# When the plain weight piece of a first-ff tile is prepared, how activations are read back, and how many dots go with a piece

## The chip, the cores and the metric

The kernel runs on one core of a Trainium2 chip. The metric is the device time of one execution in microseconds (us). Engines are named as in the profile: PE is TensorE, DVE is VectorE, ACT is ScalarE, POOL is GpSimd, SP is SyncE, which issues most of the DMAs.

## What is computed

One layer of a diffusion backbone: a half-step SwiGLU feed-forward (ff), token mixing (attention beside a long convolution), and a second half-step feed-forward, each behind an RMS norm with shift, scale and gate from a conditioning vector. The change touches the first ff, which runs on 256 latent and 256 context tokens together, and the shifts, scales and gates (the "modulation") that are worked out meanwhile. Cut to that:

```python
D_MODEL = 2048; SEQ = 256; CTX_LEN = 256; D_FF = 5632; N_MOD = 9

def swiglu(h, w_up, w_down):
    gate, up = jnp.split(h @ w_up, 2, axis=-1)
    return (jax.nn.silu(gate) * up) @ w_down

def half_ffn(s, m, slot, g, w_up, w_down):
    h = modulate(rms_norm(s, g), chunk(m, 3 * slot), chunk(m, 3 * slot + 1))
    return s + 0.5 * chunk(m, 3 * slot + 2) * swiglu(h, w_up, w_down)

mod = (s_lat @ w_ada[l] + b_ada[l])[:, None, :]
mod_c = (s_ctx @ w_ada[l] + b_ada[l])[:, None, :]
x = half_ffn(x, mod, 0, g_norm[l, 0], w_ffn1_up[l], w_ffn1_down[l])
ctx = half_ffn(ctx, mod_c, 0, g_norm[l, 0], w_ffn1_up[l], w_ffn1_down[l])
```

## The kernel before

**Precision.** Every fp32 operand x is split into a rounded part hi and the rest lo = x - hi. A product is three matmuls: hi by hi, hi by lo, lo by hi (mm3, lines 239 to 241). Weights are split as they arrive: ACT casts hi, DVE subtracts (weight(), L228 and L232; split_to(), L208 and L209).

**The up stage (Ffn.up, L445).** The 5632 columns of the first ff are 44 tiles of 128 (gate and up together). Tiles 0 to 2 are made beside the start of the kernel; the change concerns tiles 3 to 43, made one after another. A tile takes four weight pieces kq = 0 to 3 of 512 KB, four of the 16 blocks of rows each. Piece 0 is always plain: 8 products, so 24 matmuls of 512 columns. Pieces 3, 2 and 1 become "quads" from tiles 5, 7 and 9 on (QUADS): there the product of 2 x 2 blocks is made by a scheme of seven products (in place of eight) of 256 columns, 14 a piece, so 42 matmuls of 256 columns. Such a piece is split in two halves (three and four of the combined blocks), with three sums on DVE between them (L425 to L427); whi and wlo have three buffers each, raw weights four.

Piece 0 is split differently (prepare(), L412 to L420). For each half ACT casts hi (L417) and writes -hi into lo (L418), and a DMA on POOL adds the raw weight to lo in memory (L419). So DVE is not used for it. Its four result tiles come from the tag "u", a pool of 58 tiles of 256 KB that also holds the activations h (32 of them), their sums for the quads, and the results of each tile.

When a tile's products are done, they are combined and go through SiLU (L467 to L475, ACT and DVE). keep() then writes the result to memory in two parts: ACT makes a copy and its negative (L481, L482), and POOL issues two writes and an adding write (L483 to L485). All these tiles are "u" tiles too. In up(), w = self.prepare(j, kq) stands right before the matmuls of the piece:

```python
            for kq in range(4):
                w = w or self.prepare(j, kq)
                for bank, part, n, q, block, x in todo[kq]:
```

**The dots (ada_dve, L133 to L148).** The modulation needs w_ada times the conditioning vectors: 224 dots beside this ff, each a 512 KB load on SP (L141) and one multiply-and-sum on DVE (L145), or two where the context needs it too. They are dealt out by hook(): each call adds a rate to an account, and a dot is issued for each whole unit. In the up stage the hook is called after each piece (rate 0.79, from tile 4 on), in the down stage before each step (rate 1.25).

**The down stage (Ffn.down, L519).** The 44 result tiles are 11 groups of four; the 2048 output columns are 8 pieces in two passes of four. A step is one group by one piece: one weight load, one split, 24 matmuls of 512 columns. Before the four steps of a group, fetch() (L487) issues all reads of the groups up to two ahead: eight DMAs of 256 KB on POOL for each group not yet held. At most five groups are held (ROOM). In pass 1 the first steps use groups held from pass 0. The last two groups of pass 1 are made separately for the two token sets.

**Order.** The program's order is a scheduler's input: it puts instructions in the order of the program on their engines, lets later ones pass where an earlier one isn't ready, and gives buffers out tag by tag. Every engine then works through its own line in that order.

Of the kernel before, what the change touches and what calls it, by code (L numbers as in the profile page):

```python
# [12 lines left out]
F32R = mybir.dt.float32r  # L13
# [5 lines left out]
P = 128  # L19
D = 2048  # L20
KT = D // P
L = 256
FF = 5632
JT = FF // P
GRP = 4
# [6 lines left out]
WAVE = 3  # L32
ADA_UP = (5, 7, 6, 8)
ADA_DOWN = (2, 3, 4)
ADA_RATES = (0.79, 1.25)
QUADS = {3: 5, 2: 7, 1: 9}
GT = JT // GRP
PASSES = ((0, 1, 2, 3), (4, 5, 6, 7))
ORDERS = ((9, 8, 10, 7, 6, 5, 4, 3, 2, 1, 0), tuple(range(GT)))
ROOM = 5  # L40
# [22 lines left out]
def hybrid_layer_kernel(ctx: ExitStack, tc: tile.TileContext, a):  # L63
    nc = tc.nc
# [3 lines left out]
    def T(pool, shape, tag, dt=F32, bufs=None):  # L68
        serial[0] += 1
        kw = {} if bufs is None else {"bufs": bufs}  # L70
        return pool.tile(list(shape), dt, tag=tag, name=f"{tag}_{serial[0]}", **kw)
# [3 lines left out]
    up = ctx.enter_context(tc.tile_pool(name="up", bufs=1))  # L75
    pp = ctx.enter_context(tc.tile_pool(name="pp", bufs=4, space=PSUM))

    def U(shape, dt=F32):
        return T(up, shape, "u", dt, 58)

    def tmp(shape):
        return T(up, shape, "sq", bufs=2)

    def tmp2(shape):
        return T(up, shape, "sg", bufs=3)
# [99 lines left out]
    def ada_col(d):  # L185

        bank = ada_bank.pop(d)
        rows = tmp2((P, 2 * P))
        copied = S.copy(rows, bank[:, 0 : 2 * P])
        for j in range(2):  # L190
            last = PE.transpose(bank[:, (2 + j) * P : (3 + j) * P], rows[:, j * P : (j + 1) * P], ident)
        col = cols[d % 2]
        turned = bank[:, 2 * P : 4 * P].rearrange("p (j g c) -> p j c g", g=4, c=32)
        V.tensor_reduce(col, turned[:, :, 0:2, :], axis=AX.X, op=ALU.add)
        V.scalar_tensor_tensor(first_mod[:, 1, d, :], col[:, 0, :], bada1[:, d : d + 1],
                               gn[:, 0, d : d + 1].broadcast_to((P, 2)), op0=ALU.add, op1=ALU.mult)
        V.tensor_scalar(first_mod[:, 0, d, :], col[:, 1, :], bada[:, d : d + 1], None, op0=ALU.add)
        return copied, last, bank
# [39 lines left out]
    def mm3(ps, w, xx, start, stop):  # L238
        PE.matmul(ps, w[0], xx[0], start=start, stop=False)  # L239
        PE.matmul(ps, w[0], xx[1], start=False, stop=False)  # L240
        return PE.matmul(ps, w[1], xx[0], start=False, stop=stop)  # L241
# [110 lines left out]
    class Ffn:  # L352
# [89 lines left out]
                    for bank, part, block, term in terms:  # L442
                        yield bank, part, n, q, block, (2 * kq + q, term)

        def up(self, j, w=None):  # L445
            todo = [list(self.products(j, kq)) for kq in range(4)]
            left = [sum(t[0] == bank for piece in todo for t in piece) for bank in range(4)]
            total = list(left)
            banks = [(PA, PB)[j % 2]((P, 2, L)) if n else None for n in left]
            for kq in range(4):  # L450
                w = w or self.prepare(j, kq)
                for bank, part, n, q, block, x in todo[kq]:
                    ps = banks[bank] if part is None else banks[bank][:, part, :]
                    xx = self.h[x] if part is None else self.sums[x[0]][x[1]]
                    left[bank] -= 1
                    mm3(ps, [t[q][:, block] if kq == 0 else t[:, q, block] for t in w[n]], xx, left[bank] == total[bank] - 1, left[bank] == 0)
                w = None
                if j == JT - 1 and kq == 1:
                    self.fetch(ORDERS[0][0])
                self.hook()  # L460
            for kq in QUADS:
                if QUADS[kq] == j + 1:
                    self.install(kq)
            if not total[2]:
                return self.close(j, banks)
            g, v, u = tmp((P, 2, L)), U((P, 2, L)), T(up, (P, L), "mt", bufs=3)
            S.copy(g[:, 0, :], banks[2][:, 0, :])  # L467
            V.tensor_add(u, g[:, 0, :], banks[2][:, 1, :])
            V.tensor_add(g[:, 1, :], u, banks[3][:, 0, :])
            V.tensor_add(v[:, 0, :], u, banks[3][:, 1, :])  # L470
            V.tensor_add(v[:, 1, :], g[:, 1, :], banks[3][:, 1, :])
            V.tensor_add(g, g, banks[0])
            V.tensor_add(v, v, banks[1])
            S.activation(g, g, AF.Silu)
            V.tensor_mul(v, v, g)  # L475
            self.keep(j, v)
# [7 lines left out]
            nc.gpsimd.dma_start(actd[j][:, 1], minus)  # L484
            nc.gpsimd.dma_start(actd[j][:, 1], act.bitcast(F32R), accum_op=ALU.add)  # L485

        def fetch(self, g):  # L487

            if g not in self.held:
                self.held[g] = []  # L490
                for j in range(g * GRP, (g + 1) * GRP):
                    act = U((P, 2, L), F32R), U((P, 2, L), F32R)
                    for s_ in range(2):
                        nc.gpsimd.dma_start(act[s_], actd[j][:, s_])
                    self.held[g].append(act)

        def step(self, g, dq, banks, begin, end, part=None, done_=None):

# [20 lines left out]
        def down(self, after):  # L519

            uses = [(p, g) for p in range(len(PASSES)) for g in ORDERS[p]]
            for n, (p, g) in enumerate(uses):
                if g == ORDERS[p][0]:
                    banks = {2 * dq + i2: (PA, PB)[k // 2]((P, 2, L)) for k, dq in enumerate(PASSES[p]) for i2 in range(2)}
                for _, soon in uses[n : n + 3]:
                    self.fetch(soon)
                    while len(self.held) > ROOM:
                        left = [q for _, q in uses[n:]]
                        out = max(self.held, key=lambda q: left.index(q) if q in left else len(left))
                        del self.held[out]  # L530
                if g == ORDERS[p][5]:
                    for dq in PASSES[p]:
                        for i in range(2):
                            xs[i][dq] = U((P, 2, L))
                            nc.sync.dma_start(xs[i][dq], a["xT"][i, dq])
                at = n - len(uses) + APART
                if at == 0:
                    break
                for dq in PASSES[p]:
                    self.hook()  # L540
                    self.step(g, dq, banks, g == ORDERS[p][0], g == ORDERS[p][-1] or at == -1)
            yield
            rest = [g for _, g in uses[-APART:]]
            for part in (1, 0):
                banks = {dq: (PA if part else PB)((P, 2, L)) for dq in PASSES[-1]}
                for g in rest:
                    self.fetch(g)
                    for dq in PASSES[-1]:
                        self.step(g, dq, banks, g == rest[0], g == rest[-1], part, None if part else after)
                if part:  # L550
                    yield
# [7 lines left out]
    actd = [T(dram, (P, 2, 2, L), f"act{j}", F32R) for j in range(JT)]  # L559
# [108 lines left out]
    owed, rate = [0.0], [0.0]  # L668

    def ada_next():  # L670
        if done[0] < len(todo):
            c, d, b = todo[done[0]]
            ada_dve(c, d, b)
            done[0] += 1
            if b == 1:
                ada_finish(c, d, d + 1)

    def ada_hook():
        owed[0] += rate[0]
        while owed[0] >= 1.0:  # L680
            owed[0] -= 1.0
            ada_next()
# [8 lines left out]
    f1 = Ffn(a["w_up1"], a["w_dn1"], 0)  # L691
# [3 lines left out]
    w = {j: tuple(T(wp, (P, 4, 2, P), n, F32R, 3) for n in ("whi", "wlo")) for j in range(WAVE)}  # L695
# [144 lines left out]
    with tc.issue_after(mm.ins), tc.issue_after(scaled.ins), tc.issue_after(shifted.ins):  # L840
        copied, mm, _ = ada_col(1)
# [31 lines left out]
                raws = [weight_load(f1.wup[j, d // 4 + 1], (P, 4, 2, P), G) for j in range(WAVE)]  # L873
    for _ in steps:
        pass
    ahead = f1.prepare(WAVE, 0)
    for j in range(WAVE):
        f1.close(j, wave[j])
    rowp_cm.__exit__(None, None, None)
# [6 lines left out]
    f1.hook = lambda: next(build, None)  # L886
    rate[0] = ADA_RATES[0]
    for j in range(WAVE, JT):
        f1.up(j, ahead if j == WAVE else None)
        if j == WAVE:  # L890
            for i in range(2):
                crow.append(T(adap, (P, D), f"crow{i}", bufs=1))
                nc.scalar.dma_start(crow[i], a["crow"][i : i + 1, :].partition_broadcast(P))
                S.activation(crow[i], crow[i], AF.Silu)
            f1.hook = lambda: (next(build, None), ada_hook())
# [6 lines left out]

    more = mix_input(1, cont, PASSES[-1][0], PA)
    norm_plan = iter(NORM_PLAN)
    f1.hook, rate[0] = ada_hook, ADA_RATES[1]
    downs = f1.down(lambda: [next(more) for _ in range(next(norm_plan))])
    next(downs)
    while done[0] < len(todo):
# [368 lines left out]
    for b in range(NB):  # L1277
        ps, _ = out_unit(0, b)
# [26 lines left out]
    def mod_x(d, src):  # L1305
        m_ = T(up, (P, L), "mt", bufs=3)[:, 0 : src.shape[1]]
        return m_, S.activation(m_, src, AF.Identity, bias=mod[0][6][:, d : d + 1], scale=mod[0][7][:, d : d + 1])
# [47 lines left out]
    m_, _ = mod_x(0, pt[:, 0, :])  # L1355
# [16 lines left out]
    xn, _ = scaled_x(1, 0)  # L1372
# [213 lines left out]
```

## Time and profile before

| | |
|---|---|
| three runs | 3176.53 us median (3173.2 to 3181.67) |
| the profiled execution | 3183.79 us, span 3182.0 us |
| mean granted clock of PE | 0.915 |
| busy: PE, DVE, ACT, POOL | 87%, 60%, 35%, 8% |
| tile 4 begins, tile 43 begins | 186.27 us, 1504.47 us after the span's start |

The page gives, for each engine, its busy time, and in 40 equal slices the tenths of the slice in which it was busy; PEclk is the clock that the throttle granted, in tenths. A view of waits has the engine and line that waited, what released it, the sum in us, how often, and the longest. A view of stretches has for each stretch its length and each engine's busy time with the number of instructions, the mean clock, the share in which the DMA engines were busy, and GB/s. A view in order of time has start, duration, engine, line, operation, output<-inputs, and in brackets the idle time before with its releaser. PEld is PE's weight load.

### The profile page before, as it was taken

Reading aid. Unit: us, or ns where it says so; the run is one execution under the profiler, and the core shown is the slowest. Engines: PE = TensorE matmul, PEld = TensorE weight load, DVE = VectorE, ACT = ScalarE, POOL = GpSimd, SP = SyncE. Lnnn points to the kernel's source line nnn. Section 1 sums busy time; section 2 is a strip of 40 time slices with the busy share of each in tenths; the row PEclk is TensorE's granted clock in tenths of the full one; section 3 lists DMA queues with packets and bytes.
Section 4 is the critical chain, followed back from the end, with each engine's and each line's share of the span. In section 5 each row is a group of like instructions: output and inputs, shape, how many; then the busy total and the mean of one; then the engine's idle time right before and its main releaser. Section 6 shows DMA issues by size and latency. Waiting matters only on the chain.

```text
span 3182.0 us, 38107 instructions
## 1 busy us (share of the span) xinstructions
PE 2752.6 (87%) x14480; PEld 2334.4 (73%) x14480; DVE 1914.0 (60%) x3050; ACT 1124.6 (35%) x1545; POOL 254.2 (8%) x394
## 2 busy tenths in 40 slices
PE   8977776776776776776899999999999999999999
PEld 5666666675666666666677877888887888888887
DVE  6745456455455455455667877787897555545444
ACT  4433323223233233233111211455565444444333
POOL 1110101101001001101220010000000000000000
PEclk9998788888887887787999999999999999999999
DMA  9865555555555555555997687455355666666665
GB/s 372 297 195 157 142 147 153 156 145 157 145 153 150 151 146 156 145 156 160 318 352 257 232 291 256 152 179 172 106 166 172 186 189 189 191 187 191 212 200 163
DMA packets 194004, 607.91 MB, mean 191 GB/s; under 512 B 22299, under 2 KB 25308, under 8 KB 189468
## 3 DMA queue, kind: packets, MB, share of 16 engines
q1 hardware_dynamic: 140012, 501.77, 47.4%
q0 software_dynamic: 53184, 100.95, 13.6%
q10 hardware_dynamic: 624, 2.75, 0.3%
q8 instruction: 113, 1.85, 0.2%
q14 instruction: 71, 0.58, 0.1%
HBM read 545.08 MB, written 38.81 MB: 183 GB/s over the span
## 4 chain that ended last, share of the span: by engine, by line
PE 40%; issue 40%; DMA 9%; DVE 6%; POOL 4%; ACT 1%; SPq 0%; POOLq 0%; DVEq 0%; ACTq 0%
PE pa L1246 8%; PE pa L1247 8%; PE pa L1245 8%; DMA adaw<-in_w_adaT_dram 6%; PE pa L247 3%; DVE adas L145 3%; DVE wlo L232 2%; PE pa L249 1%; PE pb L241 1%; PE pb L239 1%; PE pb L240 1%; POOL act L485 1%; POOL u L419 1%; PE pa L239 1%; PE pa L241 1%
## 5 line engine op out<-in xcount | busy, mean ns | idle before, releaser
L232 DVE TENSOR_TENSOR wlo<-raw,whi 128x1024 fp32r<-128x1024 f32 x487 | 595.4, 1223 | 435.5 <-ACT whi L228 433.7
L228 ACT CAST whi<-raw 128x1024 fp32r<-128x1024 f32 x487 | 512.2, 1052 | 923.6 <-PE pa L1247 413.4
L208 ACT CAST whi<-raw 128x768 fp32r<-128x768 f32 x222 | 208.5, 940 | 723.0 <-PE pb L240 253.9
L241 PE MATMUL pb<-u,wlo 128*128 128x256 f32 (+1 forms) x1262 | 405.6, 322 | 19.2 <-DVE wlo L232 11.2
L239 PE MATMUL pa<-u,whi 128*128 128x256 f32 (+1 forms) x1252 | 411.8, 330 | 4.7 <-DMA u<-act 2.6
L1245 PE MATMUL pa<-whi,u 128*128 128x512 f32 x1060 | 413.9, 391 | 0.0
L240 PE MATMUL pa<-u,whi 128*128 128x256 f32 (+1 forms) x1252 | 407.1, 326 | 7.0 <-DMA u<-act 6.6
L1246 PE MATMUL pa<-wlo,u 128*128 128x512 f32 x1060 | 412.8, 390 | 0.2 <-DVE wlo L232 0.2
L1247 PE MATMUL pa<-whi,u 128*128 128x512 f32 x1060 | 412.8, 390 | 0.0
L239 PE MATMUL pb<-u,whi 128*128 128x256 f32 (+1 forms) x1262 | 409.4, 324 | 2.0 <-ACT whi L208 2.0
L241 PE MATMUL pa<-u,wlo 128*128 128x256 f32 (+1 forms) x1252 | 405.9, 325 | 0.0
L240 PE MATMUL pb<-u,whi 128*128 128x256 f32 (+1 forms) x1262 | 404.6, 321 | 0.0
L209 DVE TENSOR_TENSOR wlo<-raw,whi 128x768 fp32r<-128x768 f32 x222 | 241.5, 1090 | 228.8 <-ACT whi L208 228.0
L145 DVE CUSTOM_DVE_ANT_0 adas<-adaw,crow,mod 128x1024 bf16<-128x1024 f32 x160 | 205.3, 1283 | 245.1 <-DMA adaw<-in_w_adaT_dram 242.6
L145 DVE CUSTOM_DVE_ANT_0 adas<-adaw,crow,cond 128x1024 bf16<-128x1024 f32 x160 | 205.1, 1282 | 225.9 <-DMA adaw<-in_w_adaT_dram 224.0
L241 PEld LDWEIGHTS pb<-u,wlo 128*128 128x128 f32 x1262 | 245.9, 195 | 39.7 <-DVE wlo L232 22.0
L239 PEld LDWEIGHTS pa<-u,whi 128*128 128x128 f32 x1252 | 246.4, 197 | 32.5 <-issue 5.3
L240 PEld LDWEIGHTS pa<-u,whi 128*128 128x128 f32 x1252 | 244.7, 195 | 28.2 <-DMA u<-act 8.1
L239 PEld LDWEIGHTS pb<-u,whi 128*128 128x128 f32 x1262 | 248.8, 197 | 22.1 <-ACT whi L208 2.2
L240 PEld LDWEIGHTS pb<-u,whi 128*128 128x128 f32 x1262 | 246.0, 195 | 18.7 <-issue 0.4
L241 PEld LDWEIGHTS pa<-u,wlo 128*128 128x128 f32 x1252 | 244.7, 195 | 17.2
L239 PE MATMUL pb<-u,u 128*128 128x512 f32 (+1 forms) x232 | 111.0, 481 | 168.9 <-ACT u L417 168.9
(337 smaller groups left out, 3926.1 us busy)
## 6 DMA issues: line engine op xcount, KB each, us to landing
adaw<-in_w_adaT_dram SPq DMA_DIRECT2D x223, 512.0 KB, 5.1
raw<-in_w_dn_dram SPq DMA_DIRECT2D x184, 512.0 KB, 3.7
raw<-in_w_up_dram SPq DMA_DIRECT2D x176, 512.0 KB, 3.6
raw<-in_w_up1q_dram SPq DMA_DIRECT2D x164, 512.0 KB, 3.6
u<-act POOLq DMA_DIRECT2D x136, 256.0 KB, 8.1
act<-u POOLq DMA_DIRECT2D x132, 256.0 KB, 2.6
wrow<-in_w_ada_dram SPq DMA_DIRECT2D x32, 1024.0 KB, 9.4
u<-raw POOLq DMA_DIRECT2D x82, 256.0 KB, 4.0
```

Of the source, the lines that this page charges most:

```text
L145: V.tensor_tensor_reduce(out=sc, in0=t, in1=crow[i][:, b * (D // 2) : (b + 1) * (D // 2)], scale=1.0, scalar=mcol if b else bada[:, n : n ...
L208: S.copy(hi, src)
L209: V.tensor_sub(lo, src, hi.bitcast(F32))
L228: S.copy(hi, raw)
L232: V.tensor_sub(lo, raw, hi.bitcast(F32))
L239: PE.matmul(ps, w[0], xx[0], start=start, stop=False)
L240: PE.matmul(ps, w[0], xx[1], start=False, stop=False)
L241: return PE.matmul(ps, w[1], xx[0], start=False, stop=stop)
L247: PE.matmul(ps, w[0], x, start=start, stop=stop)
L1245: PE.matmul(ps[t], hi, w[0], start=start, stop=False)
L1246: PE.matmul(ps[t], hi, w[1], start=False, stop=False)
L1247: last = PE.matmul(ps[t], lo, w[0], start=False, stop=stop)
```

## The change

Three things are changed.

1. In up(), piece 0 of tile j + 1 is prepared after the matmuls of piece 1 of tile j, and kept in self.ahead. Before, it was prepared at the beginning of tile j + 1. The work itself is the same.
2. fetch() reads one tile (two DMAs) a call. In the down stage it is called once a step, for the group two ahead; before tile 43's pieces 2 and 3, two whole groups are read (before: one, after piece 1). Which group is dropped is decided in fetch(), which now protects the two groups before the one fetched.
3. The rate of dots is 1.05 a step in pass 0 and 1.4 in pass 1, in place of 1.25 in both.

```diff
-ADA_RATES = (0.79, 1.25)
+ADA_RATES = (0.79, 1.05, 1.4)
...
-        def up(self, j, w=None):
+        def up(self, j):
...
             for kq in range(4):
-                w = w or self.prepare(j, kq)
+                w = self.prepare(j, kq) if kq else self.ahead
...
-                w = None
-                if j == JT - 1 and kq == 1:
-                    self.fetch(ORDERS[0][0])
+                if j == JT - 1 and kq < 2:
+                    for n in range(GRP):
+                        self.fetch(ORDERS[0], kq, n)
+                if j < JT - 1 and kq == 1:
+                    self.ahead = self.prepare(j + 1, 0)
                 self.hook()
...
-        def fetch(self, g):
-
-            if g not in self.held:
+        def fetch(self, order, n, jj):
+
+            if n >= len(order):
+                return
+            g = order[n]
+            if jj == 0 and g not in self.held:
                 self.held[g] = []
-                for j in range(g * GRP, (g + 1) * GRP):
-                    act = U((P, 2, L), F32R), U((P, 2, L), F32R)
-                    for s_ in range(2):
-                        nc.gpsimd.dma_start(act[s_], actd[j][:, s_])
-                    self.held[g].append(act)
+                while len(self.held) > ROOM:
+                    out = max(self.held, key=lambda q: order[n:].index(q) if q in order[n:] else -1 if q in order[n - 2 : n] else len(order))
+                    del self.held[out]
+            if len(self.held[g]) == jj:
+                act = U((P, 2, L), F32R), U((P, 2, L), F32R)
+                for s_ in range(2):
+                    nc.gpsimd.dma_start(act[s_], actd[g * GRP + jj][:, s_])
+                self.held[g].append(act)
...
-                for _, soon in uses[n : n + 3]:
-                    self.fetch(soon)
-                    while len(self.held) > ROOM:
-                        left = [q for _, q in uses[n:]]
-                        out = max(self.held, key=lambda q: left.index(q) if q in left else len(left))
-                        del self.held[out]
+                order = [q for _, q in uses]
...
-                for dq in PASSES[p]:
-                    self.hook()
+                for jj, dq in enumerate(PASSES[p]):
+                    self.fetch(order, n + 2, jj)
+                    self.hook(p)
                     self.step(g, dq, banks, g == ORDERS[p][0], g == ORDERS[p][-1] or at == -1)
...
-    ahead = f1.prepare(WAVE, 0)
+    f1.ahead = f1.prepare(WAVE, 0)
...
-        f1.up(j, ahead if j == WAVE else None)
+        f1.up(j)
...
-    f1.hook, rate[0] = ada_hook, ADA_RATES[1]
+    def down_hook(p):
+        rate[0] = ADA_RATES[1 + p]
+        ada_hook()
+
+    f1.hook = down_hook
```

More of the change, by code (lines that the diff above doesn't have):

```diff
@@ L546, in down @@
                 for g in rest:
-                    self.fetch(g)
                     for dq in PASSES[-1]:
```

## Prediction

> **What bounds the kernel now.** I read the page's slices first, then the waits of TensorE (PE), then busy time by stretches, then the instructions in order of time around one tile's end.
>
> ```profile
> span 3182.0 us, 38107 instructions
> ...
> PE   8977776776776776776899999999999999999999
> ...
> DVE  6745456455455455455667877787897555545444
> ...
> PEclk9998788888887887787999999999999999999999
> ```
>
> PE is nearly full from the twentieth slice on. Before that, in the first ff's up, both its busy share and its granted clock are low, and DVE, the next busiest, is at about half. The next answer has the stage from the first matmul of tile 4 to the first of tile 43 (39 tiles), two pieces of one tile, and the three stretches of the down stage.
>
> ```profile
> core 0: us, PE busy (x) PEld busy (x) DVE busy (x) ACT busy (x) POOL busy (x), PEclk, DMA share, GB/s
> 186.27:1504.47 1318.20, 949.12 (x5688) 858.11 (x5688) 694.51 (x1146) 388.38 (x553) 147.28 (x196) 0.81 0.53 151
> 648.90:657.72 8.82, 0.18 (x2) 0.00 (x1) 7.99 (x15) 4.17 (x8) 0.83 (x2) 0.73 0.35 124
> 657.72:666.64 8.92, 8.19 (x22) 6.56 (x23) 1.15 (x3) 1.75 (x3) 2.95 (x4) 0.50 0.93 178
> ...
> 1504.47:1639.00 134.53, 116.62 (x521) 94.77 (x522) 88.47 (x149) 25.48 (x28) 44.31 (x81) 0.91 1.03 338
> 1639.00:1820.00 181.00, 175.33 (x770) 144.16 (x769) 146.84 (x219) 35.83 (x36) 12.72 (x24) 1.00 0.72 248
> 1820.00:2055.00 235.00, 227.43 (x1185) 194.50 (x1184) 169.80 (x281) 62.06 (x73) 20.11 (x38) 1.00 0.73 243
> ```
>
> A tile takes 1318.20 / 39 = 33.8 us. At its end PE stands still for 8.8 us, and then it works 8.9 us at a clock of 0.50. What it waits for in this stage:
>
> ```profile
> PE pb L239 <- ACT u L417: 168.9, 20, 11.0
> PE pa L239 <- ACT u L417: 160.2, 20, 9.0
> PE pa L241 <- DMA u<-raw: 25.1, 20, 6.9
> PE pb L241 <- DMA u<-raw: 17.6, 19, 2.4
> ```
>
> All of it is the plain piece (kq 0): 329 us for its casts on ACT and 43 us for the lo parts that POOL's adding DMA makes. Nothing else stops PE here. Why the casts are late is seen in ACT's order:
>
> ```profile
> 654.41 0.63 ACT L474 ACTIVATE sq<-sq 128x512 f32<-128x512 f32 x1 [3.74 <-DVE sq L472]
> 655.88 0.62 ACT L481 CAST u<-u 128x512 fp32r<-128x512 f32 x1 [0.84 <-DVE u L475]
> 656.53 0.63 ACT L482 ACTIVATE u<-u 128x512 fp32r<-128x512 f32 x1
> 657.07 0.60 ACT L417 CAST u<-raw 128x512 fp32r<-128x512 f32 x1
> 657.70 0.64 ACT L418 ACTIVATE u<-u 128x512 fp32r<-128x512 f32 x1
> ```
>
> L417 of the next tile comes behind L474, L481 and L482 of this tile's end, which need PE's last sums. ACT is idle for 3.74 us before, so it is not work that delays L417. Its tiles come from the tag "u", which v and the two copies in keep() share and claim earlier in the program. I take it that the tag is served in program order.
>
> **The up stage without these waits.** PE's own time follows from start-to-start distances at full clock:
>
> ```profile
> 648.32 0.28 PE L240 MATMUL pb<-u,whi 128*128 128x256 f32 x1
> ...
> 648.80 0.28 PE L241 MATMUL pb<-u,wlo 128*128 128x256 f32 x1
> ```
> ```profile
> 1699.65 0.39 PE L239 MATMUL pa<-u,whi 128*128 128x512 f32 x1
> ...
> 1706.00 0.39 PE L240 MATMUL pb<-u,whi 128*128 128x512 f32 x1
> ```
> ```profile
> 657.72 0.80 PE L239 MATMUL pa<-u,u 128*128 128x512 f32 x1 [8.64 <-ACT u L417]
> 658.31 0.63 PE L240 MATMUL pa<-u,u 128*128 128x512 f32 x1
> ...
> 659.17 0.63 PE L240 MATMUL pa<-u,u 128*128 128x512 f32 x1
> ```
>
> The first pair is 4 matmuls apart: 0.12 us for 256 columns. The second is 28 apart: 0.227 us for 512. At the clock of 0.50 it is 0.43 us (the last two rows, 2 apart). A full quad tile has 24 matmuls of 512 columns and 3 x 42 of 256: 5.45 + 15.12 = 20.57 us. A plain piece in place of a quad one costs 5.45 for 5.04, so tile 4 is 21.8, tiles 5 and 6 are 21.4 each, 7 and 8 are 21.0 each. With 34 x 20.57 the 39 tiles come to 806 us. That is 512 below 1318. The terms agree: 329 + 43 of waiting, and at half clock 8.2 us of work lose 1 - 0.227/0.43 = 47%, 3.9 us a tile, 151 us, together 523.
>
> Part one of the change moves prepare(j+1, 0) to after the second piece of tile j. All that it issues moves: one weight load on SP (now ahead of those of pieces 2 and 3), two L417 and two L418 on ACT, two L419 on POOL. The adding DMAs move ahead of L483 to L485 of keep(j) on POOL. No instruction is added. What hides them is this. ACT is busy 388 of 1318 us, 10.0 us a tile, so 10.0 of 20.6. The four casts take 2.5 us, and their room is the four tiles of piece 0 of tile j, free 5.5 us into the tile. Piece 2's second cast waits for one of three weight slots (L428) until the 18 matmuls of piece 1's first half are done, 5.45 + 18 x 0.12 = 7.6 us into the tile, and its result is needed at 5.45 + 5.04 + 2.16 = 12.7. ACT's other work there (L474, L481, L482 and the four casts, 4.4 us) can push it from 7.6 to 9.9; cast and subtraction (1.05 and 1.23 us, the rows of L208 and L209 below) end at 12.2. It fits by 0.5 us. DVE is busy 694.51 / 39 = 17.8 us a tile, 87% of 20.6.
>
> ```profile
> L208 ACT CAST whi<-raw 128x1024 fp32r<-128x1024 f32 x109 | 114.2, 1047 | 614.6 <-DVE raw L427 222.3 <-PE pb L240 192.6 <-PE pa L240 191.7
> ...
> L209 DVE TENSOR_TENSOR wlo<-raw,whi 128x1024 fp32r<-128x1024 f32 x109 | 133.5, 1225 | 189.0 <-ACT whi L208 188.7
> ...
> L145 DVE CUSTOM_DVE_ANT_0 adas<-adaw,crow,mod 128x1024 bf16<-128x1024 f32 x62 | 79.5, 1282 | 197.7 <-DMA adaw<-in_w_adaT_dram 197.3
> ...
> L145 DVE CUSTOM_DVE_ANT_0 adas<-adaw,crow,cond 128x1024 bf16<-128x1024 f32 x62 | 79.4, 1281 | 169.2 <-DMA adaw<-in_w_adaT_dram 168.9
> ```
>
> So some stalls will show. Nothing before has this stage at such a load; the nearest rows are the down stage at full clock, 1639 to 2055, where DVE is at 81% and 72% and PE idles 5.7 + 7.6 = 13.3 of 416 us, 3.2%. Bounds are 0 and the 13% of 1504 to 1639 (17.9 of 134.5). I take 3.2%: 806 / 0.968 = 833, a gain of 485. Tile 43, outside the window, loses its half clock and DMA wait too: 3.9 + 0.9 = 5.
>
> [...] In the rows, PE has been working 8.9 us and the clock is still 0.50. [...]
>
> **The down stage.** Part two reads the activations back two DMAs a step, not eight at once, and starts with two groups while tile 43 runs. Its room is h, which frees 8 tiles after each of tile 43's pieces. Part three takes dots out of pass 0 (1.25 to 1.05 a step) and puts them in pass 1 (1.4). Over 160 hooks at 0.79, 44 at 1.05 and 36 at 1.4 that is 223 of 224 dots; one is left over, 2.6 us of DVE off the path.
>
> ```profile
> PE pb L241 <- DVE wlo L232: 11.2, 7, 3.0
> ...
> PE pa L240 <- DMA u<-act: 6.6, 3, 4.0
> ...
> PE pa L239 <- DMA u<-act: 2.6, 4, 1.2
> ```
>
> In 1500 to 2060 the reads cost PE 9.2 us directly, and the mean clock of 0.91 in the first 134.5 us is 12 us of lost clock, of which half follows these waits. I take 15 for part two, between 0 (the DMA share of 1.03 stays) and 30 (17.9 idle and 12 of clock). For part three: a step is 24 x 0.227 = 5.45 us of PE. DVE needs 1.22 for L232 and two times 1.28 + 0.08 a dot: 1.22 + 1.05 x 2.72 = 4.1 in pass 0, 1.22 + 1.4 x 2.72 = 5.0 in pass 1. It fits, so I take 0; bounds are a gain of 11 (all wlo waits go) and a loss of 18 (pass 1's 36 steps, should 34 us of waits for dot loads come on top of 36 x 5.0 = 180, against 196 of PE).
>
> ```profile
> L232 DVE TENSOR_TENSOR wlo<-raw,whi 128x1024 fp32r<-128x1024 f32 x30 | 36.6, 1223 | 3.5 <-ACT whi L228 3.2 <-PE pb L241 0.3
> L145 DVE DVE_READ_ACCUMULATOR2_ANT mod<- 128x1 f32 x68 | 5.6, 83 | 0.0
> ```
>
> Sum: 485 + 5 + 15 = 505. The profiled execution took 3183.8 us (span 3182.0), 0.2% above the median of 3176.5. That gives 2679 against its own time, 2672 against the median; I say 2675.
>
> **Rivals.** *No stalls at all* (12%): 512 + 5 + 30, time 2635. For it: before, PE has no wait inside the quad pieces.
>
> *The dots' loads hold DVE* (17%). DVE waits 197.3 + 168.9 = 366 us for them in these 39 tiles, 9.4 us a tile, now in PE's idle time; a subtraction behind a waiting dot is late. With half of it left a tile takes 17.8 + 4.7 = 22.5 and the time is 2720; with all of it 27.2 and 2905. The DMA share would rise from 0.53 to about 0.84. [...] Against it: loads are issued a tile ahead, and in 1639 to 1820 a share of 0.72 costs PE 3%.
>
> *The change doesn't do what it says* (4%): the four tiles find no room before the tile's end, L417 stays where it is, and only the down stage gains, 15 us: 3165.
>
> *The half clock had cost only 1.6 us a tile* (3%): 2752, as above. The trace's 0.50 over 8.92 us speaks against it.
>
> The last rival needs these two rows, L485's issue in the tile that began at 648.9 and the median landing of such writes:
>
> ```profile
> 660.50 1.08 POOL L485 DMA_DIRECT2D act<-u  x1
> ```
> ```profile
> act<-u POOLq DMA_DIRECT2D x132, 256.0 KB, 2.6
> ```
>
> *Slower: ACT is blocked* (4%). L417 of the next tile stands in ACT's line in mid tile. If its room is that of keep(j-1), it waits for L485's landing, 660.5 - 648.9 + 2.6 = 14.2 us into the tile, and the casts of pieces 2 and 3 stand behind it. PE then stalls 6 us (12.7 to 19.0) and pays 3.9 for the clock: 30.8 a tile, still faster. It turns slower at 13.2 us a tile, when that landing comes 3 us later; with 12 us of stall a tile takes 36.5 and the time is 3290. Against it: piece 0's own room is free earlier.
>
> **How the numbers follow.** My forecast has 60%, for 2640 to 2720. From 2625 to 2790 lie it, most of the first rival and the lighter half of the second: 80%. About 0.3% is what a measurement of this kernel can tell from no change. Faster 0.95 (all but the last rival and a part of the third), same 0.02, slower 0.03.
>
> **What would show it.** The tiles' starts 21 to 21.5 us apart; no wait of L239 for L417; the granted clock of the up stage at 0.97 or more; DVE near 85% there; its DMA share near 0.85; in the down stage no waits for u<-act, and waits for wlo moved from pass 0 to pass 1. Wrong would be: waits of L241 for wlo L209 of over 2 us a tile (second rival), L417 still behind L482 (third), or ACT idle before L417 with its release by a DMA (last).

## The result and the profile after

| | before | after |
|---|---|---|
| median of the runs compared | 3179.1 us (3173.2 to 3186.49) | 2819.24 us (2815.55 to 2819.76) |
| the profiled execution, its span | 3183.79 us, 3182.0 us | 2818.97 us, 2817.2 us |
| mean granted clock of PE | 0.915 | 0.977 |

The ratio is 0.8865, with a 95% interval of 0.8843 to 0.8886. The time falls by 11%, but it is 144 us above the forecast and 29 us above the range.

The page of after, where the up stage of the first ff now ends in the seventeenth slice:

```profile
span 2817.2 us, 38140 instructions
...
PE   8999998988888889899999999999999999999999
...
DVE  6756776766776676776898879688875455554444
...
PEclk9999999999999999899999999999999999999999
```

The stretches of after, the up stage (first matmul of tile 4 to that of tile 43) and then the three of the down stage, with the columns shown before:

```profile
182.65:1162.39 979.74, 868.46 (x5689) 803.54 (x5688) 684.74 (x1131) 377.90 (x550) 147.83 (x196) 0.95 0.71 201
1162.39:1300.00 137.61, 124.26 (x585) 104.05 (x584) 95.98 (x158) 29.90 (x34) 47.36 (x88) 0.96 1.09 366
1300.00:1480.00 180.00, 179.07 (x789) 147.48 (x788) 149.51 (x225) 37.24 (x37) 11.65 (x22) 1.00 0.73 251
1480.00:1700.00 220.00, 213.82 (x1119) 183.08 (x1117) 174.16 (x294) 63.16 (x76) 16.92 (x32) 0.99 0.74 248
```

A tile takes 979.74 / 39 = 25.1 us (before 33.8, forecast 21.4), and single tiles take 20.8 to 30.1. The gain of 364.8 us in the span falls into 3.6 ahead of tile 4 (186.27 to 182.65), 338.5 in the 39 tiles (forecast 485) and 22.7 from tile 43 to the end (1677.5 to 1654.8; forecast 20). So the 39 tiles gain 147 us less than forecast, and all that is missing is missing there. What waits there (PE, DVE and ACT):

```profile
PE pa L241 <- DVE wlo L209: 29.4, 29, 3.1
PE pa L239 <- ACT whi L208: 29.0, 14, 3.2
PE pb L241 <- DVE wlo L209: 26.5, 24, 3.4
PE pb L239 <- ACT whi L208: 23.6, 16, 3.1
...
DVE adas L145 <- DMA adaw<-in_w_adaT_dram: 178.4, 62, 9.1
...
ACT whi L208 <- DVE raw L427: 241.6, 72, 8.9
ACT sq L476 <- DVE sq L474: 175.6, 35, 8.2
```

The waits for L417 are gone from PE's list. In their place are 108.5 us for the hi and lo parts of quad pieces, 83 waits of some 1.3 us. The stage's time can also be split by the distances between the matmuls' starts. The spacing of full clock (0.12 and 0.227 us) counts as work, which gives 805.8 us in every kernel with these matmuls. What a distance has beyond it counts as standing still where PE was idle for at least 0.15 us, else as half clock or as the rest. The 979.7 us then are 805.8 of work, 124.5 of standing still, 39.3 of half clock and 10.0 of the rest. Before, the last three were 386.0, 124.8 and 1.6.

**One such wait, followed back.** The rows are of after in order of time, in tile 28, which begins at 776.99: first three DMA issues on SP, then DVE, ACT and PE.

```profile
775.93 0.33 SPq L216 DMA_DIRECT2D raw<-in_w_up1q_dram  x1
776.30 0.43 SPq L141 DMA_DIRECT2D adaw<-in_w_adaT_dram  x1
776.85 0.36 SPq L216 DMA_DIRECT2D raw<-in_w_up1q_dram  x1
...
777.83 0.42 DVE L427 TENSOR_TENSOR raw<-raw 128x256 f32<-128x256 f32 x1
781.29 1.28 DVE L145 CUSTOM_DVE_ANT_0 adas<-adaw,crow,mod 128x1024 bf16<-128x1024 f32 x1 [3.03 <-DMA adaw<-in_w_adaT_dram]
782.50 0.08 DVE L145 DVE_READ_ACCUMULATOR2_ANT mod<- 128x1 f32 x1
782.50 0.42 DVE L470 TENSOR_TENSOR mt<-sq,pb 128x256 f32<-128x256 f32 x1
...
785.83 0.68 DVE L474 TENSOR_TENSOR sq<-sq,pb 128x512 f32<-128x512 f32 x1
...
779.51 0.83 ACT L208 CAST whi<-raw 128x768 fp32r<-128x768 f32 x1
786.61 0.63 ACT L476 ACTIVATE sq<-sq 128x512 f32<-128x512 f32 x1 [6.26 <-DVE sq L474]
788.35 0.62 ACT L483 CAST u<-u 128x512 fp32r<-128x512 f32 x1 [1.11 <-DVE u L477]
789.00 0.63 ACT L484 ACTIVATE u<-u 128x512 fp32r<-128x512 f32 x1
789.54 0.60 ACT L417 CAST u<-raw 128x512 fp32r<-128x512 f32 x1
790.17 0.63 ACT L418 ACTIVATE u<-u 128x512 fp32r<-128x512 f32 x1
790.71 0.60 ACT L417 CAST u<-raw 128x512 fp32r<-128x512 f32 x1
791.22 1.04 ACT L208 CAST whi<-raw 128x1024 fp32r<-128x1024 f32 x1
...
789.53 0.28 PE L241 MATMUL pa<-u,wlo 128*128 128x256 f32 x1
792.31 0.39 PE L239 MATMUL pa<-u,whi 128*128 128x256 f32 x1 [2.50 <-ACT whi L208]
```

Followed back from the last row: PE waits for the cast L208 of 791.22. ACT makes it behind the casts of the next tile's plain piece (L417, L418), which it makes behind the copies L483 and L484 of the last tile's result. Those wait for SiLU (L476), SiLU for DVE's sums (L470 to L474), and these have stood since 778.25 behind a dot that waits 3.03 us for its load, issued only at 776.30, 5.0 us before. No engine is short of time here: ACT has been idle for 6.26 us, and the DMA engines had nothing to do from 775.4 to 776.9 (below). The dot's load was issued late because it stands in SP's line behind the weight load of 775.93, and this one had waited 7.36 us for a buffer that an adding DMA set free.

```profile
DMA  9970008499999999996300093893000000598909
```

This is the window 774 to 793 us in 40 slices of 0.475 us; a zero is a slice in which they were busy less than a tenth, here the fourth to the sixth.

This is one case. Of the 62 dots that wait in the stage, 24 have a sum for a quad piece behind them as the next work other than a dot (L425 or L427), 19 an end sum (L470 or L471), 17 have the subtraction of a weight piece and two another sum. A sum of the first kind delays a weight cast directly; such waits are the first of ACT's two rows above.

**The theories.** A: dots stand in DVE's line so soon behind their loads that DVE waits at the head of its line; the tile's end sums, ACT's line and PE follow. In before such waits (366 us) would then have lain in the time in which PE waited for L417. Two reasons for "so soon" were open: SP can't issue the loads in time, because it waits for room for a weight piece (A1), or the scheduler puts the dot too early into DVE's line (A2). Rivals: DVE has too much work (87% of a 20.6-us tile); the DMA engines are full; the plain piece stands at the wrong place of ACT's line; parts two and three cost time. Baselines of the runs below are between 3175.25 and 3178.66 us.

### The profile page after: what moved, and what is told of

The parts are those of the page before. It is cut to its first block, busy times and chain, and to the rows that moved or that the text cites. A ratio compares the mean times of both kernels' runs of the same rounds, so it can differ in the third digit from the quotient of the medians.

```text
span 2817.2 us, 38140 instructions
## 1 busy us (share of the span) xinstructions
PE 2662.6 (95%) x14480; PEld 2275.9 (81%) x14480; DVE 1910.3 (68%) x3050; ACT 1116.5 (40%) x1545; POOL 253.5 (9%) x394
## 4 chain that ended last, share of the span: by engine, by line
PE 59%; issue 19%; DMA 12%; DVE 6%; POOL 2%; ACT 2%; SPq 0%; POOLq 0%; DVEq 0%; ACTq 0%
PE pa L1254 10%; PE pa L1252 10%; PE pa L1253 9%; DMA adaw<-in_w_adaT_dram 5%; DMA u<-raw 4%; PE pb L241 4%; PE pb L239 4%; PE pb L240 4%; PE pa L247 3%; PE pa L241 3%; PE pa L239 3%; PE pa L240 3%; PE pa L249 2%; DVE adas L145 1%; DMA act<-u 1%
## 5 line engine op out<-in xcount | busy, mean ns | idle before, releaser
L241 PE MATMUL pa<-u,wlo 128*128 128x256 f32 (+1 forms) x1252 | 416.0, 332 | 36.0 <-DVE wlo L209 29.4
L241 PE MATMUL pb<-u,wlo 128*128 128x256 f32 (+1 forms) x1262 | 412.9, 328 | 37.5 <-DVE wlo L209 30.6
L239 PE MATMUL pa<-u,whi 128*128 128x256 f32 (+1 forms) x1252 | 415.1, 332 | 31.1 <-ACT whi L208 29.0
L239 PE MATMUL pb<-u,whi 128*128 128x256 f32 (+1 forms) x1262 | 412.0, 327 | 25.7 <-ACT whi L208 25.7
L208 ACT CAST whi<-raw 128x768 fp32r<-128x768 f32 x222 | 205.4, 938 | 300.0 <-DVE raw L427 253.1
L241 PEld LDWEIGHTS pb<-u,wlo 128*128 128x128 f32 x1262 | 249.7, 198 | 61.8 <-DVE wlo L209 37.5
L241 PEld LDWEIGHTS pa<-u,wlo 128*128 128x128 f32 x1252 | 249.7, 199 | 61.7 <-DVE wlo L209 35.7
L239 PEld LDWEIGHTS pa<-u,whi 128*128 128x128 f32 x1252 | 249.2, 199 | 57.7 <-ACT whi L208 32.3
L239 PEld LDWEIGHTS pb<-u,whi 128*128 128x128 f32 x1262 | 249.4, 198 | 47.5 <-ACT whi L208 29.2
L240 PEld LDWEIGHTS pa<-u,whi 128*128 128x128 f32 x1252 | 249.3, 199 | 18.5 <-DVE u L789 1.5
L1253 PEld LDWEIGHTS pa<-wlo,u 128*128 128x128 f32 x1060 | 199.1, 188 | 41.5 <-DVE wlo L232 0.6
```

Source lines behind the costliest of these rows:

```text
L208: S.copy(hi, src)
L1253: PE.matmul(ps[t], hi, w[1], start=False, stop=False)
```

## The experiments

**1. The dots of the up stage without loads** (dots_noload).

```diff
-        t = T(adap, (P, D // 2), "adaw", bufs=4)
...
+        if 0 < done[0] < 126:
+            t = crow[0][:, b * (D // 2) : (b + 1) * (D // 2)]
```

> The up stage's dots keep their multiply-and-sum on DVE (1.28 us each), but read a vector that is already in memory, so that none of their 126 loads is issued and no dot can wait for one. Part of the computation is left out: those modulation values are not the reference's. Theory A (a dot whose load is late stands at the head of DVE's line and holds the end of the tile and the weight splits behind it): tiles fall from 25.1 to 21 to 21.5 us, no wait of PE for whi or wlo of more than 20 us in sum, 2660 to 2690 us. Theory B (in ACT's line the copies of keep() and the casts of the next plain piece stand ahead of piece 2's second cast whatever DVE does): tiles stay at 23.5 to 25, 2760 us or more. Theory C (DVE has too much work): as B.

Measured: 2722.88 us (one run), 33 above theory A's range. Freed of their loads, the dots were all put into the tiles up to 19. Stretches of tiles 9 to 19 and of tiles 20 to 42:

```profile
287.75:557.09 269.34, 243.47 (x1670) 225.24 (x1669) 253.72 (x444) 107.47 (x155) 41.26 (x55) 0.97 0.55 140
557.09:1060.88 503.79, 484.37 (x3453) 454.23 (x3452) 320.45 (x505) 222.20 (x322) 86.70 (x115) 1.00 0.58 157
```

The first 11 tiles take 24.5 us with DVE at 94%; the 23 tiles without a dot take 503.79 / 23 = 21.9. So without dots and loads nothing else costs more than 1.3 us a tile. Work and wait aren't told apart by it, since both are gone there.

**2. The loads without the dots' work** (loads_nodots).

```diff
+        w_ = 8 if done[0] < 126 else D // 2
...
-                out=sc, in0=t, in1=crow[i][:, b * (D // 2) : (b + 1) * (D // 2)], scale=1.0,
+                out=sc[:, 0:w_], in0=t[:, 0:w_], in1=crow[i][:, b * (D // 2) : b * (D // 2) + w_], scale=1.0,
```

> The up stage's dots keep their 512 KB loads and their place in DVE's line, but multiply and sum 8 columns of 1024, some 0.1 us for 1.28. Part of the computation is left out: those modulation values are not the reference's. Theory A: the loads are as late as before, tiles stay at 23.5 to 25 us, 2750 to 2820 us. Theory C (DVE's work): DVE falls by 4 us a tile, tiles to 21 to 21.5 us, 2660 to 2690 us. Theory B: little changes, 2780 or more.

Measured: 2842.02 us (one run), so no faster than after. Theory A had it at 2820 at most, and B's condition is met too; run 5 tells these two apart. Its up stage but for the last 3.5 us, and DVE's wait (line numbers are one higher):

```profile
182.43:1175.00 992.57, 877.21 (x5668) 811.38 (x5666) 557.26 (x1126) 374.69 (x550) 148.14 (x196) 0.94 0.68 198
```
```profile
DVE adas L146 <- DMA adaw<-in_w_adaT_dram: 243.8, 66, 7.2
```

A dot of 8 columns takes 0.22 to 0.23 us, where some 0.1 had been expected. DVE has 127 us less to do (557.26 for 684.74), and a tile takes 25.5 us: the wait has grown from 178.4 to 243.8 us and eaten the work saved. That DVE has too much work is out.

**3 and 4. One part at a time** (part1_alone, part23_alone). The first has before with nothing but the preparation moved, the second has the whole diff of the change without these lines, so only the new fetch() and the new rates.

```diff
-                w = w or self.prepare(j, kq)
+                w = self.prepare(j, kq) if kq else self.ahead
...
+                if j < JT - 1 and kq == 1:
+                    self.ahead = self.prepare(j + 1, 0)
```

> Only the plain piece of the next tile is prepared in mid tile; fetch and dots as in the kernel before. The up stage as in the changed kernel (25.1 us a tile), the down stage as before, some 20 us longer than in the changed kernel: 2835 to 2845 us. Were the spread reads and the dots' rates what limits or helps the up stage, it would differ from the changed kernel by more.

> Only the spread reads and the new rates of dots; the plain piece is prepared at its tile's beginning as before. Up stage as before (33.8 us a tile); the down stage gains the 20 us that it gained in the changed kernel: 3150 to 3165 us. If that gain came from the up stage's end, 3179.

Measured: part one 2834.65 us, ratio 0.8926 (0.89 to 0.8952); parts two and three 3160.33 us, ratio 0.995 (0.993 to 0.9969). Part one alone has tiles of 25.0 us and a wait of DVE for the loads of 175.7 us, so the loss belongs to it and not to the other parts. From tile 43 on it gains 5.5 us (1677.5 to 2830.5 - 1158.54 = 1672.0), and after gains 17.2 more. (The two groups that are read ahead are read behind tile 43's pieces 0 and 1, so ahead of pieces 1 and 2.)

**5. The dots pinned** (pinned). Each dot of the up stage is put on DVE behind the subtraction of the last weight piece prepared ahead of it in the program. Loads, work and everything else stay.

```diff
-            V.tensor_sub(lo, raw, hi.bitcast(F32))
+            last_lo[0] = V.tensor_sub(lo, raw, hi.bitcast(F32))
...
+    def pinned_hook():
+        with tc.issue_after(last_lo[0].ins):
+            ada_hook()
...
-            f1.hook = lambda: (next(build, None), ada_hook())
+            f1.hook = lambda: (next(build, None), pinned_hook())
```

> The changed kernel, with each dot of the up stage put into DVE's line behind the subtraction of the weight piece of its own place in the program; its load is issued where it was, so that it has about a piece's time more to land. Nothing is left out and no load is earlier. Theory A (late dot loads at the head of DVE's line): DVE's waits for adaw in the up stage fall from 178 us to under 40, tiles to 21.3 to 22.3 us, 2690 to 2730 us. Theory B (ACT's line alone) and theory D (the DMA engines are too full, so that loads are late whatever waits for them): tiles stay above 24, 2790 us or more.

Measured: 2645.68 us (2644.0 and 2647.36), ratio to before 0.8329 (0.8305 to 0.8353): 174 us less than after (170 by the two ratios) and 44 below the range expected. Of the 175.0 us between the two spans, 163 lie in the 39 tiles and 12 behind them. The stretch of its up stage, and the order of time in a tile that begins at 771.52 (line numbers from the helpers on are two higher):

```profile
182.55:999.33 816.78, 811.99 (x5689) 763.13 (x5688) 682.35 (x1127) 378.55 (x551) 147.59 (x196) 1.00 0.83 242
```
```profile
772.16 0.42 DVE L472 TENSOR_TENSOR mt<-sq,pb 128x256 f32<-128x256 f32 x1
...
774.15 0.69 DVE L476 TENSOR_TENSOR sq<-sq,pb 128x512 f32<-128x512 f32 x1
...
777.15 1.28 DVE L145 CUSTOM_DVE_ANT_0 adas<-adaw,crow,mod 128x1024 bf16<-128x1024 f32 x1
...
777.27 0.62 ACT L485 CAST u<-u 128x512 fp32r<-128x512 f32 x1 [0.63 <-DVE u L479]
```

A tile takes 20.9 us, PE stands still for 5.3 us in the whole stage, and no dot waits. The first end sum comes 0.6 us after the tile's beginning, not 5.5, and the dot behind it starts without a wait. DVE and ACT have the same work (682 and 379 us), the same loads and the same order of L417 behind the copies, and the DMA share is 0.83. So neither DVE's work, nor full DMA engines, nor L417's place cost the 174 us. What changed can be counted: from the issue of the n-th dot's load to the start of the n-th dot it is 8.4 us in the median in after, and 5.2 or less for a tenth of them; in pinned it is 16.4 us, and 11.6 or less for a tenth; in before it was 5.9. How long such a load takes to land is in the DMA issues of after's up stage (count, KB each, median us to landing):

```profile
adaw<-in_w_adaT_dram SPq DMA_DIRECT2D x124, 512.0 KB, 6.7
```

So in after a good part of the dots, 62, reaches the head of DVE's line before its load has landed, and in pinned none.

**6, 7 and 8. SP's room for weight pieces, and the loads' place** (raw0_own, pinned_raw0, free_loads). The first gives piece 0's raw weights a buffer of their own (and takes one from the dots' loads); the second adds the pin to it; the third lifts the order of the dots' loads behind the weight loads.

```diff
-        t = T(adap, (P, D // 2), "adaw", bufs=4)
+        t = T(adap, (P, D // 2), "adaw", bufs=3)
...
-        raw = T(wp, shape, "raw", bufs=4)
+        raw = T(adap, shape, "raw0", bufs=1) if own else T(wp, shape, "raw", bufs=4)
...
-            raw = weight_load(self.wupq[j - WAVE, kq], (P, 2, 4, P))
+            raw = weight_load(self.wupq[j - WAVE, kq], (P, 2, 4, P), own=kq == 0 and j > WAVE)
```
```diff
-            with tc.issue_after(last_load[0].ins):
-                nc.sync.dma_start(t, src)
+            nc.sync.dma_start(t, src)
```

> Piece 0's raw weights get a buffer of their own (the dots' loads give up one of four), so that no load on SP waits behind a piece that only the adding DMA sets free. Theory A1 (the dots' loads are late because SP stands at a weight load whose buffer waits for that adding DMA): tiles fall to 22 to 23 us, 2720 to 2760 us. Theory A2 (they are late because DVE takes them too early in its line, or because three buffers are too few): no gain, 2810 us or more.

> Both: dots behind their piece's subtraction, and piece 0's raw weights in a buffer of their own. If theory A1 is the larger part, this is better than either by 10 us or more (2680 to 2710); if the place in DVE's line is enough, it equals the first of the two within 10 us.

> The dots' loads are no longer held behind the weight load of their place, so that loads and dots can run as far ahead as four buffers allow. Theory A: no dot is late by SP's order, but more dots fall into the up stage while it lasts, 8 or more a tile, and DVE is then full: tiles of 25 us at first and 22 once the dots are done, 2700 to 2760 us in all. Theory D (full DMA engines): 2810 us or more.

Measured, one run each: raw0_own 2818.95 us, with 25.1 us a tile and 185.4 us of waiting for the loads, as after. This doesn't decide on A1, because the edit left the wait in SP's line: the new buffer is itself free only when the adding DMA of the last piece 0 has landed. In the stage SP's weight loads wait 338.5 us in 47 times for such a DMA, in after 309.5 us in 42. What the runs do show is that the cure needs no other order on SP: in pinned these waits are still 273.8 us in 43 times, and no dot waits. pinned_raw0 2651.86 us: the pin alone does it, with or without that buffer. free_loads 2871.22 us, slower than after, which theory A had not foreseen: it was to be 2700 to 2760. Theory D's 2810 or more is met in number, but the DMA share of that stage is 0.79, below pinned's 0.83. DVE does 900 us of work in that up stage (after 685), because the loads of the down stage's dots came forward, with their dots. PE then waits mostly for the adding DMA (line numbers are one lower):

```profile
PE pb L240 <- DMA u<-raw: 54.0, 18, 5.5
PE pa L240 <- DMA u<-raw: 49.1, 17, 6.3
```

So an earlier load doesn't help by itself; its dot goes forward with it (for the up stage's own dots the distance from load to dot is 9.5 us in the median, for 8.4 in after). Why the adding DMAs come so late there stays open.

**9. The pin without the change** (pin_before), the same edit as in 5 on the kernel before.

> The kernel before with nothing but the dots of the up stage pinned: each is put on DVE behind the subtraction of the last weight piece prepared ahead of it in the program. Piece 0 is still prepared at its own tile's beginning. Theory (a dot taken early costs only where nothing else stands still): in before DVE's waits for the dots' loads lie in the time in which PE waits for L417, so the pin alone is worth almost nothing, 3165 to 3185 us, up stage 33.5 to 34 us a tile, with the waits of L239 for L417 still at about 320 us. Rival (the early dots had cost before, too, and pinning is a gain of its own, 4 to 5 us a tile): 3000 us or less.

Measured: 3159.59 us, ratio 0.9939 (0.992 to 0.9959). PE's waits in tiles 4 to 41, and DVE's longest in the same stretch:

```profile
PE pa L241 <- ACT u L419: 157.5, 19, 9.6
PE pb L241 <- ACT u L419: 156.2, 19, 9.6
```
```profile
DVE wlo L211 <- ACT whi L210: 543.9, 94, 16.3
```

The pin removes the dots' waits here too, and yet the tile takes 33.6 us (33.8). The median falls by 19 us, 5 more than the range expected; of the 25.3 us between the two spans 1.8 lie ahead of tile 4, 9.4 in the up stage and 14.0 from tile 43 on. The 366 us that DVE waited in before were nearly free, and the 178 in after are not: the price of this wait comes from part one. What gives the 14.0 us behind tile 42 isn't shown.

**10. The old rates** (pinned_oldrates).

```diff
-ADA_RATES = (0.79, 1.05, 1.4)
+ADA_RATES = (0.79, 1.25, 1.25)
```

> The pinned kernel with the old rates (0.79, then 1.25 in both passes), so without part three. The prediction gave part three 0, between a gain of 11 and a loss of 18: this kernel then lies between 2628 and 2657 us, and I expect 2642 to 2652. The waits of PE for wlo of the down stage move from pass 1 to pass 0.

Measured: 2655.01 us, ratio 0.835 (0.8331 to 0.8369), 9 us above pinned (7 by the ratios), with intervals that overlap a little; 3 us more than expected. The first two stretches of the down stage, of pinned and then of this kernel:

```profile
999.33:1137.00 137.67, 133.63 (x640) 110.65 (x639) 105.86 (x176) 32.88 (x36) 50.53 (x94) 1.00 1.12 384
1137.00:1317.00 180.00, 178.67 (x785) 146.84 (x785) 150.55 (x225) 36.28 (x36) 9.53 (x18) 1.00 0.74 256
```
```profile
999.10:1137.00 137.90, 130.53 (x613) 108.43 (x612) 114.22 (x194) 31.76 (x35) 45.78 (x85) 0.96 1.09 378
1137.00:1317.00 180.00, 174.10 (x765) 142.84 (x764) 147.66 (x222) 34.78 (x35) 13.21 (x25) 1.00 0.74 257
```

PE is idle 8 us longer in these two, and the clock is 0.96 in the first. The waits for wlo don't move from pass 1 to pass 0, as had been expected: they are 1.3 to 1.5 us longer in each. So part three seems to be worth some 10 us, near the upper bound of what I gave it.

**11. The down stage's dots pinned too** (pinned_all).

```diff
         rate[0] = ADA_RATES[1 + p]
-        ada_hook()
+        pinned_hook()
```

> The pinned kernel with the down stage's dots pinned as well, each behind the subtraction of the step before. Theory: in the down stage the same thing happens on a small scale, PE waits 11.4 us for wlo there, so 2634 to 2646 us with those waits below 4 us. Rival: the waits there come from the order of ACT's and DVE's other work at the stage's beginning, and the pin changes nothing: 2642 to 2652, waits as before.

Measured: 2629.45 us, ratio 0.8278 (0.8257 to 0.8298), the fastest of all, 16 us below pinned and 190 below after; it is 5 us better than the range expected. Its first two stretches:

```profile
998.00:1137.00 139.00, 138.86 (x673) 117.21 (x672) 110.97 (x182) 33.98 (x37) 44.73 (x83) 1.00 1.11 384
1137.00:1317.00 180.00, 180.00 (x796) 149.05 (x795) 146.53 (x219) 37.35 (x37) 15.32 (x29) 1.00 0.81 271
```

PE is busy 318.9 of 319.0 us at a DMA share of 1.11 and 0.81; no wait for a dot's load is left among DVE's longest (pinned: 73.5 us), and PE's waits for wlo fall from 11.4 us to 3.0. So a DMA share above 1 alone doesn't explain the 13% that PE lost in this stretch of before, at a share of 1.03.

**12. Piece 0 prepared after piece 2** (pinned_kq2).

```diff
-                if j < JT - 1 and kq == 1:
+                if j < JT - 1 and kq == 2:
                     self.ahead = self.prepare(j + 1, 0)
```

> The pinned kernel with piece 0 of the next tile prepared after piece 2 in place of piece 1. It separates two readings of where the place of the preparation counts. If any place ahead of the tile's last sums will do as long as the dots are held (theory), the tiles stay at 20.6 to 21.0 us and the time is 2640 to 2660. If the middle of the tile is needed (rival: piece 0's loads and its adding DMAs come too late by half a tile), PE waits for raw or L417 at each tile's start, 1 us or more a tile: 2690 or more.

Measured: 2650.26 us, ratio 0.8336 (0.8316 to 0.8356), with tiles of 20.6 to 21.0 us once all pieces are quads, but for two neighbours of 18.5 and 23.0 that pinned has too: the same as after piece 1. With the dots held, the place within the tile doesn't matter between these two.

## Why the prediction was right in direction and wrong in size

**Right: the floor and what lay above it.** A full quad tile was to take 20.57 us of PE and the stage 806. In pinned most tiles take 20.58 to 20.7 us and the stage takes 816.8. The waits for L417 and for piece 0's adding DMA are gone, as forecast, and with them most of the half clock (125 us to 39). The forecast had the half clock of before at 151 us and the waits at 372; by the matmuls' starts it was 125 and 386, so the sum hardly changes (511 for 523). That the tag "u" is served in program order, taken on trust, isn't contradicted: L417 follows L484 without idle time, so nothing but its place in ACT's line is seen to hold it.

**Right: the rest of the sum.** Tile 43 was to give 5 and gave 5.5 (run 3, from tile 43 on). The down stage was to give 15 and gave 17.2. Its split was off: part three was taken at 0, and run 10 speaks for about 10, so part two gave some 7, if the two add up.

**Wrong: the step "I take 3.2%".** Measured is 1 - 805.8 / 979.7 = 17.8%, above even the upper bound of 13%. I had taken the down stage as "the nearest rows" because of DVE's busy share. What costs here isn't DVE's share: it is lower than forecast (684.74 of 979.74, 70%), and it is 84% in pinned, which loses nearly nothing. In the down stage of after a weight part stands right behind 40 of 42 waiting dots. In the up stage it is a quad piece's sum or one of the tile's end sums behind 43 of 62; the weight casts that PE needs within the same tile wait for the first directly, and for the second by way of ACT's copies and the next plain piece's casts. So one wait goes through three lines. The rows that were near were those of the dots themselves, quoted in the same part: 366 us of waits, a gap without a price so long as PE stood still.

**The second rival was the right one, at the wrong price.** "With half of it left" was met nearly exactly: 178.4 of 366 us, 4.6 a tile. But I added this to DVE's work (17.8 + 4.7 = 22.5), as if DVE set the tile's length. It doesn't: in 2, with 127 us less of DVE's work, the tile takes as long. The price is what the delay does further on: PE's 125 us of standing still and 39 of half clock in the stage, where the forecast had 27 us for everything. "Loads are issued a tile ahead" was the argument against it, and it is false: a dot starts 8.4 us (median) after its load's issue, a third of a tile, and a tenth of them within 5.2. I had not measured this distance; in before's trace it is 5.9 us.

**"It fits by 0.5 us".** ACT's line was worked out for sums on time. In pinned they are, and PE waits 1.9 us for a cast in the whole stage. In tile 28 of after, piece 2's second cast begins 14.2 us into the tile, not by 9.9.

**The half clock and the other signs.** The forecast took 3.9 us a tile for it from the rows; measured is 124.8 / 39 = 3.2. No run shows the 1.6 us a tile of the rival with 3%: before has 39 stretches at a clock of 0.50 in the 39 tiles, 31 of them 13.65 us long (last section). Of the forecast's signs, the clock of the up stage is 0.95 and not 0.97, the DMA share 0.71 and not 0.85; pinned has 1.00 and 0.83. The sign named for the second rival (waits of L241 for wlo above 2 us a tile) came out at 55.9 / 39 = 1.4, and with those of L239 for whi at 2.8.

**Not seen.** The other rivals didn't come: no wait of ACT for L485's landing, no tile takes above 30.1 us, and the moved casts did find room.

What stays open: why the scheduler puts a dot that close behind its load, whether loads that SP issues in time would do as much as the pin (A1), and why the adding DMAs are late in free_loads.

## What to carry to other kernels

A wait in an idle time had next to no price here until that idle time was taken away (the pin took 366 us of waits from before and gained 19 us, and 178 us from after and gained 174): before a stall is removed, look at what else waits inside it and what stands behind that waiting instruction on its engine and on the next ones. Where a scheduler orders the engines, measure the distance from each load's issue to its first use, against the time that such loads take to land; side work whose load may be late belongs behind the instructions that the main path needs, and here pinning it there saved 174 us of 2819 without any change of the work. Don't add a wait to an engine's work to get a stage's length when that engine isn't full (here DVE, busy 70% of after's up stage: 22.5 us a tile by that sum, 25.1 measured); follow the delay through the lines behind it.

## What the runs showed of the hardware

Behind a gap of 2.50 us PE's clock fell from 1.00 to 0.50 for 6.83 us. This is the gap before 792.31 in after, shown above:

```profile
792.30:795.70 3.40, 2.63 (x12) 2.43 (x13) 3.29 (x4) 1.21 (x2) 1.77 (x2) 0.56 0.82 112
795.70:799.00 3.30, 3.30 (x17) 3.30 (x17) 1.65 (x2) 1.55 (x2) 0.00 (x0) 0.50 1.02 284
```

The clock's record has the fall at 792.68, so before the next gap (0.76 us, from 792.81 on). In the 39 tiles there are 22 such stretches in after, 16 of 3.41 us and 6 of 6.83, and 39 in before, of which 31 last 13.65 us and begin some 2 to 5 us into gaps of mostly 8.6 us. All their lengths are multiples of 3.41. The up stages of both were cut along these stretches into pieces of 3.41 us, with PE's busy share in each (as the trace models it). In the two together, the clock falls behind 61 pieces in which PE was busy 0 to 48%, and stays at 1.00 behind 439 of 48 to 100%. It stays at 0.50 behind 113 pieces of 0 to 80% and comes back behind 61 of 84 to 100%. Around the beginning of tile 18 of before, for one, the pieces at 0.50 are 0, 61, 79 and 100% busy, and the clock of 1.00 is back behind the last:

```profile
652.96:656.37 3.41, 0.00 (x0) 0.00 (x0) 3.41 (x8) 1.12 (x2) 0.00 (x0) 0.50 0.64 262
656.37:659.79 3.42, 2.07 (x5) 1.70 (x6) 2.47 (x5) 3.03 (x6) 2.00 (x3) 0.50 0.50 153
659.79:663.20 3.41, 2.69 (x11) 2.20 (x10) 0.00 (x0) 0.00 (x0) 1.78 (x2) 0.50 1.03 159
663.20:666.61 3.41, 3.41 (x10) 2.64 (x9) 0.00 (x0) 0.00 (x0) 0.00 (x0) 0.50 0.89 149
```

These are counts from the two traces, of before and after; what else the clock depends on isn't shown.

The DMA share was 1.11 in pinned_all in a stretch in which PE was busy 99.9% of the time (138.86 of 139.00 us): there a share above 1 was no sign that transfers set the pace.
